# A decoder layer whose linear-attention values and gates become four Strassen column pairs

## The chip, the cores and the metric

The kernel runs on 1 core of one Trainium2 chip. The metric is the device time of one execution in microseconds (us).

## What is computed

One layer of a decoder trunk, 256 tokens, width 2048, all in float32. The input is normed and multiplied by one wide matrix `w_in`; its columns are the linear attention's parts, three groups of dilated attention and two gates.

```
h = RMSNorm(x)
z = h @ W_in          # GLA q, k (1024 each), v, output gate (2048 each), low-rank decay input (16),
                      # 9 x 1024 for the dilated groups, 2 x 2048 branch gates
A = GLA(q, k, v, log_sigmoid(lr @ w_gk_up + b_gk) / 16)      # 4 heads, dk 256, dv 512, chunks of 64
A = RMSNorm(A, per head) * silu(g)
Bm = DilatedAttn(h)                                           # 8 heads x 128 in 3 groups
x = x + (sigmoid(ga) * (A @ W_a) + sigmoid(gb) * (Bm @ W_b)) @ W_out
x = x + SwiGLU(RMSNorm(x))
out = RMSNorm(x)
```

## The kernel before

Every large product is done in float32 accuracy from a high and a low half: ScalarE rounds a piece of the weights to its high half `wh`, VectorE subtracts for the low half `wl` (`split`, L283), and TensorE adds three matmuls, high x high, high x low and low x high. The activations `h` are kept split in the same way (`HiLo`), transposed, in 16 k tiles of 128. 

The work is a list of jobs (`Job`, added by `win` and `add`), each a product of the 256 tokens with some columns of a weight matrix over all 16 k tiles. A job is cut into units, one weight DMA each, 1 MB as a rule, on SP's queue into a ring of three `raw` tiles; a unit is cut into sub-steps, each one split and its matmuls (`mains`). The main loop (L1105) takes the sub-steps in order: it issues the split four sub-steps ahead (`LA`, five ring pairs `wh`, `wl`), then the evacuation of the job that has just ended (`pending.evac`), then the job's hook for this sub-step (`pre`), one step of the side queue (`advance`), the sub-step's matmuls, and one more step of the side queue. So the order on each engine is fixed in program order.

The side queue holds generators, the attention heads above all (`gla_head`, L515; `dil_head`, L660): each `yield` hands the engine back to the main loop, so a head's matmuls stand between those of the jobs. `drain(tag)` runs the queue until no generator of that tag is left.

Kinds of job: "T" has the activations as the stationary operand and 512 (or fewer) weight columns moving, two token halves, 2 x 3 matmuls per k tile. "F" and "G" have the weights stationary and give a transposed result. "S" (`add_steps`, `step_mains`) takes two blocks of 512 columns at once, and two k tiles per step: a normal step is 8 products of 128 tokens x 512 columns (24 matmuls); a step listed in `fast` needs 7 products (21 matmuls) by Strassen's algorithm in Winograd's form, at the price of sums of weight blocks (`sums`, tile `t`) and of activation blocks (the forms, `x1_forms`). Before the change only the feed-forward part has "S" jobs: ten pairs of gate and up columns with steps 2, 4 and 6 of 8 fast.

Around the change the list of jobs runs (L742 to L763): the gate columns of heads 2 and 3 with the 16 low-rank columns behind them, 1040 columns as three "T" jobs of 348, 346 and 346; k and q of heads 2 and 3 ("F"); the values of heads 2 and 3; then the gates of heads 0 and 1, under which heads 2 and 3 run (tag "A"); k and q of heads 0 and 1; their values; then the dilated groups' jobs, under which heads 0 and 1 run (tag "B") and the bias table. The first job's sub-steps also stand among the transposes of the prologue (L1090), as x arrives in eight pieces.

Lines that the steps below name: L356 the matmuls of "T" and "F" jobs (L332 and L335 of "G"), L236 those of "S" jobs, L133 every ScalarE activation, L296 and L289 VectorE's part of a split, L195 to L199 its sums of weight blocks, L959 to L973 the sums at the end of an "S" job, L423 the prologue's transposes, L520 and L575 matmuls of a linear-attention head.

Of the kernel before, what the change touches and what calls it, by code (L numbers as in the profile page):

```python
# [10 lines left out]
F32 = mybir.dt.float32  # L11
# [12 lines left out]
NEG = -1e30  # L24

# [21 lines left out]
class Job:  # L47
# [14 lines left out]
    def __init__(self, kind, w, row0, nkt, col0, ncols, ktu, acts, evac, pre=None, pairs=None,  # L62
                 col1=None, fast=(), forms=None, turn=0):
        self.pairs = pairs
        self.col1, self.fast, self.forms = col1, fast, forms
        self.bank, self.turn = {}, turn
# [6 lines left out]
def trunk_layer(ctx: ExitStack, tc: tile.TileContext, x, attn_norm, w_in, w_gk_up, b_gk, gla_norm,  # L73
# [114 lines left out]
    def sums(sub):  # L188

        if sub.get("src") not in ("t13", "t24"):  # L190
            return
        b = raw_step(sub["unit"])
        if sub["src"] == "t13":
            t = sub["unit"]["t"] = env["fp"].tile([P, 4, 512], F32, name="t", tag="t")
            nc.vector.tensor_sub(t[:, 0:2], b[:, :, 1], b[:, 0])  # L195
        else:
            t = sub["unit"]["t"]
            nc.vector.tensor_sub(t[:, 2], b[:, 1, 1], t[:, 0])
            nc.vector.tensor_sub(t[:, 3], b[:, 1, 0], t[:, 2])  # L199
# [99 lines left out]
    def mains(sub, only=None, part=None):  # L299
# [6 lines left out]
        if not hasattr(job, "acc"):  # L306
# [146 lines left out]
    def view(key, slot, a, fresh=True):  # L453

        if key not in env:
            env[key] = block("z", slot).rearrange("p (a t) -> p a t", a=a)
        return env[key]
# [14 lines left out]
    def g_chunk(lo, hi, slots, base):  # L472

        def go(job):
            for a in range(2):
                c = lo
                while c < hi:
                    sc = env["rstd"][:, a:a + 1]
                    if c >= 1024:
                        act(lrn[:, a], job.acc[a][:, c - lo:hi - lo], AF.Copy, scale=sc)  # L480
                        c = hi
                        continue
                    j = c // 512
                    e = min(hi, (j + 1) * 512)
                    g = view(("g", base + j), slots[j], 2)
                    act(g[:, a, c - j * 512:e - j * 512], job.acc[a][:, c - lo:e - lo],
                                         AF.Silu, scale=sc)
                    c = e
        return go
# [10 lines left out]
    def evac_zf(key, slot):  # L500
        def go(job):
            scaled(job, view(key, slot, 4), "R")
        return go
# [11 lines left out]
    def gla_head(h, half):  # L515
# [94 lines left out]
        hl = hl_block("o", {2: 4, 3: 6, 0: 0, 1: 2}[h])  # L610
# [125 lines left out]
    def start_half(tag, heads):  # L736
        def go():
            for h in heads:
                push(tag, gla_head(h, tag))
        return go  # L740

    c0 = C_G + 1024  # L742
    for lo, hi in ((0, 348), (348, 694), (694, 1040)):
        ev = g_chunk(lo, hi, (0, 1), 2)
        if hi == 1040:
            def ev(job, f=ev):
                f(job)
                push("A", gla_lr())
        win("T", c0 + lo, hi - lo, ev)
    win("F", C_K + 512, 512, evac_zf(("k", "A"), 2))  # L750
    win("F", C_Q + 512, 512, evac_zf(("q", "A"), 3))
    win("T", C_V + 1024, 512, evac_t(("v", 2), 4))
    win("T", C_V + 1536, 512, evac_t(("v", 3), 5, start_half("A", (2, 3))))
    win("T", C_G, 512, g_chunk(0, 512, (6, 7), 0))
    win("T", C_G + 512, 512, g_chunk(512, 1024, (6, 7), 0))
    win("F", C_K, 512, evac_zf(("k", "B"), 8))
    win("F", C_Q, 512, evac_zf(("q", "B"), 9), {0: lambda: drain("A")})
    win("T", C_V, 512, evac_t(("v", 0), 0))

    def after_b():  # L760
        start_half("B", (0, 1))()
        push("bias", bias_table())
    win("T", C_V + 512, 512, evac_t(("v", 1), 1, after_b))  # L763


# [117 lines left out]
    FAST = (2, 4, 6)  # L883
    x1F = {}

    def x1_forms():

        yield from idle(1)
        for n, st in enumerate(FAST):
            t = x1T[st // 2].t[st % 2]  # L890
            a = env["fp"].tile([P, 2, S], F32, name="fa", tag="u0")
            f = env["fp"].tile([P, 4, P], F32, name="ff", tag="u1")
            nc.vector.tensor_add(a, t[:, :, 0].bitcast(F32), t[:, :, 1].bitcast(F32))
            nc.vector.tensor_add(f[:, 0], a[:, 0, P:], a[:, 1, P:])
            nc.vector.tensor_sub(f[:, 2], a[:, 0, 0:P], a[:, 0, P:])
            nc.vector.tensor_sub(f[:, 1], f[:, 0], a[:, 0, 0:P])
            nc.vector.tensor_sub(f[:, 3], a[:, 1, 0:P], f[:, 1])
            b = x1F[st] = block("o", n, F32R).rearrange("p (w f q) -> p w f q", w=2, f=4)
            act(b[:, 0], f, AF.Copy)
            nc.vector.tensor_sub(b[:, 1], f, b[:, 0].bitcast(F32))  # L900
            yield
            yield

    def ffn_norm_chunk(c):
# [5 lines left out]
        if c == 3:  # L910
# [3 lines left out]
            push("F", x1_forms())  # L914

    def evac_out(c):
        def go(job):
            for a in range(2):
                nc.vector.tensor_add(x1[c][:, a], job.acc[a], x1[c][:, a])
                junk = env["fp"].tile([P, 512], F32, name="junk", tag="u3")  # L920
# [33 lines left out]
    def evac_step1(job):  # L954

        u = job.u = [env["fp"].tile([P, 512], F32, name=f"u{i}", tag=f"u{i}") for i in range(4)]
        b = job.bank
        act(u[0], b["p1"], AF.Copy)
        nc.vector.tensor_add(u[1], u[0], b["p6"])  # L959
        nc.vector.tensor_add(u[2], u[1], b["p7"])  # L960
        nc.vector.tensor_add(u[1], u[1], b["p5"])
        nc.vector.tensor_add(u[3], u[2], b["p5"])

    def evac_step2(p):
        def go(job):
            u, b = job.u, job.bank
            z = env["fp"].tile([P, 2, 512], F32, name="sg", tag="sg", bufs=2)
            nc.vector.tensor_add(z[:, 0], u[0], b["p2"])
            act(z[:, 0], z[:, 0], AF.Silu, scale=env["rstd2"][:, 0:1])
            nc.vector.tensor_add(u[1], u[1], b["p3"])  # L970
            nc.vector.tensor_add(z[:, 1], u[2], b["p4"])
            act(z[:, 1], z[:, 1], AF.Silu, scale=env["rstd2"][:, 1:2])
            nc.vector.tensor_add(u[3], u[3], b["p8"])  # L973
            for a in range(2):
                nc.vector.scalar_tensor_tensor(z[:, a], u[1 + 2 * a], env["rstd2"][:, a:a + 1], z[:, a],
                                               op0=ALU.mult, op1=ALU.mult)
            turn_up(p, z, 2, 2 * job.turn)
        return go

    def evac_down(c, last):  # L980
        def go(job):
            for a in range(2):
                nc.vector.tensor_add(x1[c][:, a], job.acc[a], x1[c][:, a])
                if last:
                    junk = env["fp"].tile([P, 512], F32, name="junk", tag="u3")
# [13 lines left out]
    def fast_pair(p, turn):  # L999
        def start():  # L1000
            drain("F")
            drain("A")
        job = Job("S", w_ffn_in, 0, KT, 512 * p, 512, 2, x1_acts, evac_step2(p), {4: start}, None,
                  FF + 512 * p, FAST, lambda st: x1F[st], turn)
        add(job)
        job.pre[len(job.subs) - 2] = lambda: evac_step1(job)
# [26 lines left out]
    more = next(i for i, s in enumerate(subs) if s["job"].kind == "S") + LA + 1  # L1033
# [47 lines left out]
    def input_rstd():  # L1081
# [5 lines left out]
        env["R"] = row_bcast("R", env["rstd"])  # L1087

# [116 lines left out]
```

## Time and profile before

| | |
|---|---|
| median of 3 runs | 1864.06 us (1863.65 to 1865.05) |
| profiled execution | 1863.59 us, span 1861.5 us |
| TensorE (PE) busy | 1847.5 us, 9234 matmuls |
| VectorE (DVE) busy | 1197.6 us |
| ScalarE (ACT) busy | 913.2 us |
| granted TensorE clock, mean | 0.999 |

The span runs from the first to the last instruction of the profiled execution. Matmuls are pipelined: one's duration reaches into the next one's, so what a matmul costs in a row of them is the distance from its start to the next start, and of n equal matmuls that a row merges, (row's time - one's duration) / (n - 1). `x8` at a row's end is the number of instructions, a timeline's row begins with start and time in us, `[... <-X]` is what ended an engine's idle time before it.

### The profile page before, as it was taken

How to read it: one execution, taken by the hardware profiler on the slowest of the kernel's cores; microseconds unless marked ns; L12 is line 12 of the kernel's file. 1: busy time of each engine (PE TensorE's matmuls, PEld its weight loads, DVE VectorE, ACT ScalarE, POOL GpSimd, SP SyncE). 2: the span in 40 equal slices, each digit the busy share in tenths (PEclk: the TensorE clock that was granted, in tenths of full speed). 3: DMA queues.
4: the chain of work that ended last, by engine and by line, in shares of the span. 5: the costliest groups of instructions: out<-in, count | busy, mean ns of one | idle time of the engine just before them, and what ended most of it. 6: DMA issues, size and time to landing. Idle time of an engine off the chain costs nothing.

```text
span 1861.5 us, 23268 instructions
## 1 busy us (share of the span) xinstructions
PE 1847.5 (99%) x9234; PEld 1572.2 (84%) x9234; DVE 1197.6 (64%) x1394; ACT 913.2 (49%) x1144; POOL 22.3 (1%) x35
## 2 busy tenths in 40 slices
PE   8999999999999999999999999999999999999998
PEld 8988988888888888888888888888888888888887
DVE  6446646745665466655545556789647998559974
ACT  6446545544444444544444455555435555335553
POOL 0000000000000000000000000000000000000001
PEclk9999999999999999999999999999999999999999
DMA  7554455455555566466656655555655655545562
GB/s 253 205 195 167 159 187 176 162 182 186 179 176 181 192 182 209 147 199 207 205 201 218 234 182 180 192 193 204 219 188 189 217 183 205 201 161 203 202 236 103
DMA packets 208580, 356.33 MB, mean 191 GB/s; under 512 B 7403, under 2 KB 67879, under 8 KB 208472
## 3 DMA queue, kind: packets, MB, share of 16 engines
q1 hardware_dynamic: 203472, 346.19, 54.1%
q0 software_dynamic: 1728, 5.51, 1.4%
q10 hardware_dynamic: 3272, 3.16, 0.6%
q8 instruction: 72, 1.18, 0.2%
q14 instruction: 36, 0.29, 0.0%
HBM read 352.70 MB, written 2.13 MB: 191 GB/s over the span
## 4 chain that ended last, share of the span: by engine, by line
PE 99%; DMA 0%; DVE 0%; ACT 0%; SPq 0%; issue 0%; DVEq 0%; ACTq 0%
PE acc L356 51%; PE acc L236 12%; PE acc L332 10%; PE psb L356 6%; PE psa L236 5%; PE acc L335 5%; PE psb L236 5%; PE psa L672 1%; PE psb L717 0%; PE psa L593 0%; PE psa L818 0%; PE psb L575 0%; PE psb L682 0%; PE psb L719 0%; PE acc L818 0%; PE psa L693 0%
## 5 line engine op out<-in xcount | busy, mean ns | idle before, releaser
L133 ACT ACTIVATE wh<-raw 128x1024 fp32r<-128x1024 f32 (+3 forms) x614 | 625.8, 1026 | 633.6 <-PE acc L356 435.6
L296 DVE TENSOR_TENSOR wl<-raw,wh 128x1024 fp32r<-128x1024 f32 (+2 forms) x482 | 580.9, 1212 | 505.7 <-ACT wh L133 503.8
L356 PE MATMUL acc<-wh,h 128*128 128x512 f32 (+2 forms) x1536 | 469.8, 383 | 0.0
L356 PEld LDWEIGHTS acc<-wh,h 128*128 128x128 f32 x1536 | 286.6, 188 | 54.2 <-issue 1.3
L356 PE MATMUL acc<-wl,h 128*128 128x512 f32 (+2 forms) x768 | 292.9, 381 | 0.0
L332 PE MATMUL acc<-h,wh 128*128 128x512 f32 x768 | 196.4, 397 | 0.0
L356 PE MATMUL acc<-wh,z 128*128 128x512 f32 x600 | 187.8, 390 | 0.0
L289 DVE TENSOR_TENSOR wl<-raw,wh 128x1024 fp32r<-128x1024 f32 (+1 forms) x132 | 143.1, 1100 | 42.3 <-ACT wh L133 41.9
L356 PEld LDWEIGHTS acc<-wl,h 128*128 128x128 f32 x768 | 144.7, 188 | 25.5
L332 PEld LDWEIGHTS acc<-h,wh 128*128 128x128 f32 x768 | 138.5, 189 | 26.9 <-issue 0.7
L236 PE MATMUL acc<-wh,h 128*128 128x512 f32 x446 | 146.7, 390 | 0.0
L356 PEld LDWEIGHTS acc<-wh,z 128*128 128x128 f32 x600 | 112.6, 188 | 23.2
L356 PE MATMUL acc<-wl,z 128*128 128x512 f32 x300 | 116.7, 389 | 0.0
L335 PEld LDWEIGHTS acc<-h,wl 128*128 128x128 f32 x768 | 104.6, 190 | 7.8
L335 PE MATMUL acc<-h,wl 128*128 128x256 f32 x768 | 106.9, 282 | 0.0
L236 PEld LDWEIGHTS acc<-wh,h 128*128 128x128 f32 x446 | 83.7, 188 | 17.3
L356 PE MATMUL acc<-h,wh 128*128 128x256 f32 x512 | 92.5, 283 | 0.0
L236 PE MATMUL acc<-wl,h 128*128 128x512 f32 x223 | 86.8, 389 | 0.0
L133 ACT ACTIVATE wh<-t 128x1024 fp32r<-128x1024 f32 x51 | 54.1, 1060 | 58.4 <-DVE t L199 26.5
L356 PEld LDWEIGHTS acc<-h,wh 128*128 128x128 f32 x512 | 80.0, 192 | 0.2
L356 PE MATMUL acc<-wh,o 128*128 128x512 f32 x256 | 79.4, 389 | 0.0
L356 PE MATMUL psb<-wh,z 128*128 128x512 f32 (+1 forms) x248 | 75.8, 381 | 0.0
(276 smaller groups left out, 2308.6 us busy)
## 6 DMA issues: line engine op xcount, KB each, us to landing
raw<-in_w_in_dram SPq DMA_DIRECT2D x144, 1024.0 KB, 4.7
raw<-in_w_ffn_in_dram SPq DMA_DIRECT2D x160, 512.0 KB, 4.4
raw<-in_w_ffn_out_dram SPq DMA_DIRECT2D x44, 1024.0 KB, 5.0
raw<-in_w_branch_gla_dram SPq DMA_DIRECT2D x16, 1024.0 KB, 5.0
raw<-in_w_out_dram SPq DMA_DIRECT2D x16, 1024.0 KB, 4.9
raw<-in_w_branch_dil_dram SPq DMA_DIRECT2D x8, 1024.0 KB, 4.9
raw<-in_w_ffn_in_dram SPq DMA_DIRECT2D x8, 1024.0 KB, 4.7
raw<-in_w_in_dram SPq DMA_DIRECT2D x8, 692.0 KB, 4.0
```

The source lines that it names most:

```text
L133: nc.scalar.activation(o, i, func, **kw)
L236: nc.tensor.matmul(job.bank[pr["b"]], st, mv, start=pr["first"] and i == 0, stop=pr["last"] and i == 2, skip_group_check=True)
L289: nc.vector.tensor_sub(wl, src, wh.bitcast(F32))
L296: nc.vector.tensor_sub(wl[:, :k * n], src, wh[:, :k * n].bitcast(F32))
L332: nc.tensor.matmul(job.acc[j], wh[:, kk, c], hl.both(aj), start=ki == 0, stop=ki == job.nkt - 1, skip_group_check=True)
L335: nc.tensor.matmul(job.acc[j][:, 0:S], wl[:, kk, c], hl.hi(aj), start=False, stop=ki == job.nkt - 1, skip_group_check=True)
L356: nc.tensor.matmul(dst, st, mv, start=first and i == 0 and j % per_bank == 0, stop=last and i == 2, skip_group_check=True)
L672: nc.tensor.matmul(p1[:, g * 256:(g + 1) * 256], qk[g][:, 0, 128:256], qk[g][:, 1], start=g != 1, stop=True, skip_group_check=True)
```

## The change

The gates and the values of the linear attention, 4 x 1024 columns, become four "S" jobs (`win_fast`), each a pair of two heads' 512 columns, with steps 2, 4 and 6 of 8 fast as in the feed-forward part. The forms of h that they need (`act_forms`) are made once, under the second job. The 16 low-rank columns get a "T" job of their own: one unit, one sub-step, 16 k tiles x 2 token halves x 3 matmuls of 16 columns. The order is now: k, q of heads 2 and 3; low-rank; gates of heads 2 and 3, gates of heads 0 and 1, values of heads 2 and 3, values of heads 0 and 1; k, q of heads 0 and 1. Heads 2 and 3 start when the last value pair is done and run under k and q of heads 0 and 1 and the first dilated jobs; heads 0 and 1 start under the dilated jobs as before. Tiles in `z` and `o` get other places. The feed-forward part's "S" jobs are built by the same helper (`fast_job`): the sums of a pair's end stand in another order, two sums are made in place, and the weight sums live in two tiles `t13` and `t24` instead of one.

```diff
+    def act_forms(blocks, out, dst, tmp):
+        yield from idle(1)
+        for n, st in enumerate(FAST):
...
+            nc.vector.tensor_add(a, t[:, :, 0].bitcast(F32), t[:, :, 1].bitcast(F32))
+            nc.vector.tensor_add(f[:, 0], a[:, 0, P:], a[:, 1, P:])
+            nc.vector.tensor_sub(f[:, 2], a[:, 0, 0:P], a[:, 0, P:])
+            nc.vector.tensor_sub(f[:, 1], f[:, 0], a[:, 0, 0:P])
+            nc.vector.tensor_sub(f[:, 3], a[:, 1, 0:P], f[:, 1])
...
+            act(b[:, 0], f, AF.Copy)
+            nc.vector.tensor_sub(b[:, 1], f, b[:, 0].bitcast(F32))
+            yield
+            yield
+    def fast_job(w, col0, col1, acts, forms, turn, tile, dst, evac, pre):
+        def first(job):
+            c = job.c = dst()
+            b = job.bank
+            act(c[0], b["p1"], AF.Copy)
+            nc.vector.tensor_add(c[1], c[0], b["p6"])
+            nc.vector.tensor_add(c[2], c[1], b["p7"])
+            nc.vector.tensor_add(c[1], c[1], b["p5"])
+            nc.vector.tensor_add(c[3], c[2], b["p5"])
+        def second(job):
+            for i, n in ((0, "p2"), (2, "p4"), (1, "p3"), (3, "p8")):
+                nc.vector.tensor_add(job.c[i], job.c[i], job.bank[n])
+                evac(job, i)
+        job = Job("S", w, 0, KT, col0, 512, 2, acts, second, pre, None, col1, FAST, lambda st: forms[st], turn, tile)
+        add(job)
+        job.pre[len(job.subs) - 2] = lambda: first(job)
...
-        add(Job(kind, w_in, 0, KT, col, n, 8 if n <= 256 else 4, h_acts, evac, pre))
+        add(Job(kind, w_in, 0, KT, col, n, KT if n < 64 else 8 if n <= 256 else 4, h_acts, evac, pre))
...
+        def evac(job, i):
+            act(job.c[i], job.c[i], func, scale=env["rstd"][:, i // 2:i // 2 + 1])
+            if then and i == 3:
+                then()
+        fast_job(w_in, col, col + 512, h_acts, hF, turn, lambda t: block("o", int(t == "t24")), dst, evac, pre)
...
-    for lo, hi in ((0, 348), (348, 694), (694, 1040)):
...
-    win("F", C_K + 512, 512, evac_zf(("k", "A"), 2))
-    win("F", C_Q + 512, 512, evac_zf(("q", "A"), 3))
-    win("T", C_V + 1024, 512, evac_t(("v", 2), 4))
-    win("T", C_V + 1536, 512, evac_t(("v", 3), 5, start_half("A", (2, 3))))
-    win("T", C_G, 512, g_chunk(0, 512, (6, 7), 0))
-    win("T", C_G + 512, 512, g_chunk(512, 1024, (6, 7), 0))
-    win("F", C_K, 512, evac_zf(("k", "B"), 8))
-    win("F", C_Q, 512, evac_zf(("q", "B"), 9), {0: lambda: drain("A")})
-    win("T", C_V, 512, evac_t(("v", 0), 0))
-    win("T", C_V + 512, 512, evac_t(("v", 1), 1, after_b))
+    win("F", C_K + 512, 512, evac_zf(("k", "A"), 6))
+    win("F", C_Q + 512, 512, evac_zf(("q", "A"), 7))
+    win("T", C_LR, 16, evac_lr)
+    win_fast("g", (2, 3), (3, 5), C_G + 1024, 0, AF.Silu, {4: first_fast})
+    win_fast("g", (0, 1), (8, 9), C_G, 1, AF.Silu, {})
+    win_fast("v", (2, 3), (2, 4), C_V + 1024, 0, AF.Copy, {})
+    win_fast("v", (0, 1), (0, 1), C_V, 1, AF.Copy, {}, last_values)
+    win("F", C_K, 512, evac_zf(("k", "B"), ("o", 0)))
+    win("F", C_Q, 512, evac_zf(("q", "B"), ("o", 1), after_b))
...
+            if r == 0:
+                first = {3: lambda g=g: drain(("A2", "A2", "A3")[g])}
...
-    more = next(i for i, s in enumerate(subs) if s["job"].kind == "S") + LA + 1
+    more = next(i for i, s in enumerate(subs) if s["job"].w is w_ffn_in and s["job"].kind == "S") + LA + 1
```

`more` is the place from which on every sixth sub-step's split goes to a sixth pair of buffers; it stays in the feed-forward part.

TensorE's order, the gate columns of heads 2 and 3 before (`h_168` and the like are split tiles of h, `acc` a bank of PSUM):

```order
L356 MATMUL acc<-wl,h_168 128x346
L356 MATMUL acc<-wh,h_168 128x346 x2
L356 MATMUL acc<-wl,h_168 128x346
L356 MATMUL acc<-wh,h_168 128x346
L356 MATMUL acc<-wh,h_169 128x346
```

and now, at the end of the low-rank job and the start of the first pair (L272 is the matmul of an "S" job in the changed kernel, L392 that of the others):

```order
L392 MATMUL acc<-wh,h_319 128x16 x2
L392 MATMUL acc<-wl,h_319 128x16
L392 MATMUL acc<-wh,h_319 128x16
L272 MATMUL acc<-wh,h_119 128x512
L272 MATMUL acc<-wl,h_119 128x512
L272 MATMUL acc<-wh,h_119 128x512 x2
```

The 16 low-rank columns, which were part of the 346 wide matmuls, are now 96 matmuls by themselves ahead of the first pair.

ScalarE's order at that place now (`lrn` is the normed low-rank input, copied out of the bank):

```order
L134 ACTIVATE wh<-raw 128x1024 x2
L134 ACTIVATE wh<-raw 128x512
L134 ACTIVATE lrn<-acc,r_attn 128x16 x2
L134 ACTIVATE wh<-raw 128x1024
L537 COPY lrT<-psb 16x256
```

The copies stand behind the split of 512 columns for the first fast step. Before, they stood between the evacuations of a gate job.

VectorE's order at the end of the last value pair now (`z_2153` and `z_2154` hold the values of heads 0 and 1):

```order
L332 TENSOR_TENSOR wl<-raw,wh 128x1024 x2
L240 TENSOR_TENSOR z_2153<-z_2153,psa 128x512
L240 TENSOR_TENSOR z_2153<-z_2153,psb 128x512
L240 TENSOR_TENSOR z_2154<-z_2154,psa 128x512
L240 TENSOR_TENSOR z_2154<-z_2154,psb 128x512
L332 TENSOR_TENSOR wl<-raw,wh 128x1024
L553 SCALAR_TENSOR_TENSOR gk<-psb,ge 128x512
```

and TensorE's there (L544 is head 2's first matmul):

```order
L272 MATMUL psb<-wl,h_319 128x512
L272 MATMUL psb<-wh,h_319 128x512
L392 MATMUL acc<-h_119,wh 128x256 x2
L392 MATMUL acc<-h_119,wl 128x256
L544 MATMUL psb<-lrT,wgk 128x256 x2
L392 MATMUL acc<-h_120,wh 128x256 x2
```

Between the pair's last matmul and head 2's first stand the 24 matmuls of one sub-step of k; both sides use the banks `psb`.

## Rows read from the trace of the kernel before

**Rows 1.** The page: span, busy time by engine.
```profile
span 1861.5 us, 23268 instructions
...
PE 1847.5 (99%) x9234; PEld 1572.2 (84%) x9234; DVE 1197.6 (64%) x1394; ACT 913.2 (49%) x1144; POOL 22.3 (1%) x35
```
**Rows 2.** All waits of TensorE: what waited, for what, us in total, times, longest.
```profile
PE psb L1027 <- DMA grow<-in_attn_norm_dram: 3.8, 1, 3.8
PE psb L423 <- DMA o<-in_x_dram: 1.5, 1, 1.5
```
**Rows 3.** L356 from 38 to 54 us: count, shortest/median/longest ns, first and last start.
```profile
L356 PE MATMUL acc<-wh,h x69: 316/322/330, 37.7 to 53.9; 128*128 128x346 f32 x69
...
L356 PE MATMUL acc<-wl,h x34: 316/322/329, 37.9 to 53.6; 128*128 128x346 f32 x34
```
**Rows 4.** 512-column job's timeline; four pairs' busy (PE, PEld, DVE, ACT, POOL).
```profile
104.51 0.62 PE L356 MATMUL acc<-wh,h 128*128 128x512 f32 x2
...
114.04 0.62 PE L356 MATMUL acc<-wh,h 128*128 128x512 f32 x2
...
1403.40:1571.70 168.30, 168.30 (x756) 139.64 (x755) 149.87 (x165) 95.01 (x104) 0.00 (x0) 1.00 0.57 198
```
**Rows 5.** L575, a head's small matmuls: timeline, then durations of loads and matmuls.
```profile
162.48 1.06 PE L575 MATMUL psb<-qe,ke 128*128 128x128 f32 x8
...
163.92 0.68 PE L575 MATMUL psb<-qe,kd 128*64 128x64 f32 x8
...
L575 PEld LDWEIGHTS psb<-qe,ke x32: 187/192/192, 162.3 to 343.8; 128*128 128x128 f32 x32
L575 PE MATMUL psb<-qe,ke x32: 271/275/275, 162.5 to 343.9; 128*128 128x128 f32 x32
L575 PEld LDWEIGHTS psb<-qe,kd x32: 132/138/138, 163.9 to 345.0; 128*64 128x64 f32 x32
L575 PE MATMUL psb<-qe,kd x32: 222/222/270, 163.9 to 345.0; 128*64 128x64 f32 x32
```
**Rows 6.** Busy by engine, clock, DMA share, GB/s from 4 to 7 us; DMA issues.
```profile
4.00:7.00 3.00, 1.38 (x6) 0.92 (x6) 0.92 (x3) 1.51 (x3) 0.00 (x0) 1.00 1.01 327
...
T<-ftab ACTq DMA_DIRECT2D x8, 384.0 KB, 5.8
```
**Rows 7.** ScalarE by form: count, busy us, mean ns of one, idle before.
```profile
L133 ACT ACTIVATE wh<-raw 128x512 fp32r<-128x512 f32 x30 | 18.6, 622 | 13.2 <-PE psb L356 5.0 <-PE acc L236 4.7 <-PE psb L236 3.5
...
L133 ACT ACTIVATE lrn<-acc,r_attn 128x16 f32<-128x16 f32 x2 | 0.5, 274 | 0.0
```
**Rows 8.** VectorE's timeline at the end of a feed-forward pair.
```profile
1274.42 1.22 DVE L289 TENSOR_TENSOR wl<-raw,wh 128x1024 fp32r<-128x1024 f32 x1
1275.56 0.68 DVE L968 TENSOR_TENSOR sg<-u,psa 128x512 f32<-128x512 f32 x1
...
1277.95 1.41 DVE L975 SCALAR_TENSOR_TENSOR sg<-u,r_ffn,sg 128x512 f32<-128x512 f32 x2
```
**Rows 9.** TensorE's timeline at both ends, its weight loads, clock behind its last matmul.
```profile
6.83 1.09 PE L423 MATMUL psb<-ident,o 128*128 128x128 f32 x4 [1.49 <-DMA o<-in_x_dram]
...
8.43 0.79 PE L356 MATMUL acc<-wh,h 128*128 128x348 f32 x2
...
12.36 0.48 PE L356 MATMUL acc<-wh,h 128*128 128x348 f32 x2
...
7.50 0.34 PEld L356 LDWEIGHTS acc<-wh,h 128*128 128x128 f32 x1
...
10.22 0.19 PEld L356 LDWEIGHTS acc<-wl,h 128*128 128x128 f32 x1
...
1852.64 0.28 PE L356 MATMUL psa<-wh,z 128*128 128x256 f32 x1
...
1853.00:1856.50 3.50, 0.00 (x0) 0.00 (x0) 2.22 (x9) 1.64 (x5) 0.00 (x0) 1.00 0.00 0
1856.60:1861.00 4.40, 0.00 (x0) 0.00 (x0) 0.39 (x1) 0.00 (x0) 0.00 (x0) 0.50 0.63 238
```

More of the change, by code (lines that the diff above doesn't have):

```diff
@@ L62, in __init__ @@
     def __init__(self, kind, w, row0, nkt, col0, ncols, ktu, acts, evac, pre=None, pairs=None,
-                 col1=None, fast=(), forms=None, turn=0):
+                 col1=None, fast=(), forms=None, turn=0, tile=None):
         self.pairs = pairs
         self.col1, self.fast, self.forms = col1, fast, forms
-        self.bank, self.turn = {}, turn
+        self.bank, self.turn, self.tile = {}, turn, tile
         self.kind, self.w, self.row0, self.nkt = kind, w, row0, nkt
@@ L470, in trunk_layer, with evac_lr @@
     nc.vector.memset(inside[:, ::64], 0.0)
[L472 to L489, printed above, removed]
+    def evac_lr(job):
+        for a in range(2):
+            act(lrn[:, a], job.acc[a], AF.Copy, scale=env["rstd"][:, a:a + 1])
+        push("L", gla_lr())
     def evac_t(key, slot, then=None):
@@ L498, in evac_t, with evac_zf @@
         return go
-    def evac_zf(key, slot):
+    def evac_zf(key, slot, then=None):
         def go(job):
             scaled(job, view(key, slot, 4), "R")
+            if then:
+                then()
         return go
@@ new lines, in start_half, with win_fast, dst @@
+    def start_half(half, heads):
+        for h in heads:
+            push(f"{half}{h}", gla_head(h, half))
+    hF = {}
+    def win_fast(name, heads, slots, col, turn, func, pre, then=None):
+        def dst():
+            v = [view((name, h), slot, 2) for h, slot in zip(heads, slots)]
+            return [v[i % 2][:, i // 2] for i in range(4)]
+        def evac(job, i):
+            act(job.c[i], job.c[i], func, scale=env["rstd"][:, i // 2:i // 2 + 1])
+            if then and i == 3:
+                then()
+        fast_job(w_in, col, col + 512, h_acts, hF, turn, lambda t: block("o", int(t == "t24")), dst, evac, pre)
@@ L766, in push_heads, with drain_b @@
+    win_fast("g", (0, 1), (8, 9), C_G, 1, AF.Silu, {})
[3 more added lines that the diff above has]
+    win("F", C_Q, 512, evac_zf(("q", "B"), ("o", 1), after_b))
+    def drain_b():
+        for t in ("B0", "B1", "bias"):
+            drain(t)
     def push_heads(r):
@@ L952, in evac_fup @@
         return go
[L954 to L978, printed above, removed]
     def evac_down(c, last):
@@ L1002, in start, with tile, dst, evac @@
             drain("A")
[L1003 to L1006, printed above, removed]
+        def tile(name):
+            return env["fp"].tile([P, 1024], F32, name=name, tag=name)
+        def dst():
+            z = env["sg"] = env["fp"].tile([P, 2, 512], F32, name="sg", tag="sg", bufs=2)
+            u = [env["fp"].tile([P, 512], F32, name=f"u{i}", tag=f"u{i}") for i in range(2)]
+            return z[:, 0], u[0], z[:, 1], u[1]
+        def evac(job, i):
+            a = i // 2
+            r = env["rstd2"][:, a:a + 1]
+            if i % 2 == 0:
+                act(job.c[i], job.c[i], AF.Silu, scale=r)
+                return
+            nc.vector.scalar_tensor_tensor(job.c[2 * a], job.c[i], r, job.c[2 * a], op0=ALU.mult, op1=ALU.mult)
+            if a:
+                turn_up(p, env["sg"], 2, 2 * turn)
+        fast_job(w_ffn_in, 512 * p, FF + 512 * p, x1_acts, x1F, turn, tile, dst, evac, {4: start})
     def down(p0, n, last):
```

72 lines of the change are left out of this document (26 added, 46 removed).

## The prediction

> **What bounds the kernel now.** I read the page first: TensorE is busy 1847.5 of 1861.5 us, VectorE 64% and ScalarE 49% of them [rows 1]. A busy share counts pipelined matmuls as whole, so the second view is TensorE's waits: the whole list is two, 3.8 and 1.5 us, both for DMAs in the first 7 us [rows 2]. Behind them TensorE never waits for anything, not even under the linear attention's heads. So the third view is the distance from one matmul's start to the next, on the timeline; the kernel's time is the number of matmuls times that distance, plus the start and some 9 us after the last matmul. VectorE and ScalarE make the splits that TensorE consumes, and matter only where they come late.
>
> The profiled execution took 1863.59 us, 0.47 under the median of the three runs (1864.06). I sum differences against it and put them on the median. A measurement here can tell about 0.2% (3.7 us) from no change.
>
> **Distances.** 346 columns: 69 + 34 = 103 matmuls start between 37.7 and 53.9 us, 16.2 / 102 = 0.159 us each [rows 3]. 512 columns: 42 matmuls start from 104.51 up to 114.04, in groups of three, 9.53 / 42 = 0.227 [rows 4]. The slope between 346 and 512 columns is (0.227 - 0.159) / 166 = 0.41 ns per column, the remainder 17 ns.
>
> **What goes and what comes.** The order shows it exactly: 192 matmuls of 346 and 96 of 348 columns go, 156 of 512 and 96 of 16 columns come; all other shapes keep their number.
> - Gone: 288 x 0.159 = 45.8 us.
> - Come, wide: without Strassen 192 would be needed for what the 288 did; 12 fast steps save 3 each. 156 x 0.227 = 35.4 us.
> - Come, narrow: 96 matmuls of 16 columns for the low-rank input, which used to ride along in the 346 wide ones. Each has a full 128x128 stationary tile, and each matmul of this kernel has a weight load of its own (9234 and 9234 [rows 1]). No row shows a full tile against so few columns. By its columns alone, 17 ns and 16 x 0.41, one takes 0.024; at the other end it can't be slower than a 346-wide one at the same clock, 0.159. Nearest by the stationary tile are the heads' 128-column matmuls: eight last 1.06 us, (1.06 - 0.275) / 7 = 0.112 apart; with a 64-column tile against 64 columns eight last 0.68, (0.68 - 0.222) / 7 = 0.065 [rows 5]. In these rows tile and columns shrink together. But the weight load itself lasts 192 ns for 128 columns and 138 for 64 [rows 5], 54 ns more for 64 more, so a full tile takes about 108 ns to stream, and the next load starts when the matmul before it starts. I take 0.112: 10.8 us.
>
> Sum: -45.8 + 35.4 + 10.8 = **+0.4 us**. The narrow job eats what the pairs save; the balance would be even at 0.108 per narrow matmul.
>
> **What lies around it.**
> - Start. The first job now has 512 columns where it had 348, so its first unit of two k tiles is 512 KB (2 x 128 x 512 x 4 bytes) instead of 348 and stands in SP's queue ahead of the x piece on which TensorE waits its 1.5 us. DMA moved 327 GB/s there [rows 6]: 164 KB more is +0.5 us (0 to 1). Later units are larger too, but a sub-step of the first job then takes 24 matmuls of 256 columns (0.017 + 256 x 0.00041 = 0.12 us each, 2.9 in all) instead of 12 x 0.159 us, so TensorE needs them later.
> - The low-rank input's one DMA brings 64 bytes per row in 2048 pieces; it is issued three units ahead, some 14 us of matmuls, while the nearest, 384 KB in 1 KB pieces, landed in 5.8 us [rows 6]. Nothing.
> - First pair. Its second product waits for the bank that the low-rank job leaves; the order puts the two copies that empty it behind a split of 512 on ScalarE: 0.62 + 2 x 0.27 = 1.16 us [rows 7], against 3 x 0.227 = 0.68 of the first product. +0.5 (0 to 1).
> - The pairs' VectorE work. In the four feed-forward pairs VectorE was busy 149.87 of 168.30 us without TensorE waiting [rows 4]. The new pairs ask for less: no gated product (1.41 us a pair [rows 8]) and no transposed block to split. They lack the sixth pair of split buffers that the feed-forward part borrows. A fast step needs 1.22 + 2 x 0.68 for its sums and 0.68 + 3 x 1.22 for its splits, 6.9 us by duration, against 21 matmuls, 4.8 us; but the normal step beside it needs 2.4 against 5.4, so four sub-steps of lead carry it. Nothing; what it costs without that lead is a rival. The forms of h (three times five short sums and two long ones) fall under the second job, where VectorE has 1.22 us of work per 2.9: nothing. ScalarE's table loads get fewer: nothing, it is hidden.
> - Heads. 21 steps each, two per sub-step: the A heads need 42 and get 16 + 16 under K and Q, and 10 of the 48 under the first six dilated jobs; the B heads and the bias table fit in the rest and the next values job. So no drain empties a queue at one go, and SP's and POOL's queues are passed by nothing that matters. But head 2's first matmul stands behind the first sub-step of K (2.9 us) and needs a bank that the last pair's second group of sums empties: behind one split 1.22 + 4 x 0.68 = 3.9 us [rows 8]. +1.0 (0 to 2).
> - The feed-forward sums are only reordered, same number: nothing. The same for the rest behind it.
>
> Sum at a steady clock: 0.4 + 0.5 + 0.5 + 1.0 = +2.4 us.
>
> **The clock.** In the narrow job TensorE streams 16 columns every 0.112 us, about 7 ns of them (0.41 a column), for 11 us on end. Nothing in the trace before is so thin for more than a microsecond, and the granted clock is 1.00 from 10 us to the end of the matmuls. It does move twice. At the start two 348-column matmuls take 0.79 us at 8.43 and 0.48 at 12.36: 1.2, then 2.4 GHz; ahead of the rise TensorE had done transposes, and from 7.5 on dense matmuls [rows 9]. After the last matmul (1852.64) the granted clock is still 1.00 up to 1856.5, and 0.50, 1.2 GHz, behind it [rows 9]. Weight loads are slower at the low clock too: 0.34 us at 7.50 against 0.19 at 10.22 [rows 9]. Whether so thin a stretch counts as work no row tells. I hold it for likelier than not that it doesn't: what the rise followed was full streaming. Price, with the delays of these rows: about 3.7 us of the job, 33 matmuls, at full speed, 63 at 2 x 0.112 = 14.1 us, so 17.8 instead of 10.8, +7.0; then the first pair begins at half speed for some 2.7 us (as from 7.50 to 10.22), +1.3; the first pair's wait (0.5) vanishes in it. Bounds: +3 if the fall comes late in the job; +13 if the whole job and the stretch behind it are slow. Sum: 2.4 - 0.5 + 8.3 = +10.2.
>
> The Trainium skill (TensorE: Matmul & The Clock Gate, "A second HAM failure mode: psum-queue depth-cycling") tells of a kernel whose many short pauses between matmuls, none long, were enough to send the clock back and forth. By it the fall would come, with the +10.2 above; by the granted clock of this trace, never below 1.00 between its ends, the sum would stay at +2.4.
>
> **Forecast and rivals.**
> - A, forecast, 0.50: narrow job at one weight load per matmul and the clock falls in it: 1864.06 + 10.2 = **1874.3 us** (its own range 1867 to 1879).
> - B, 0.31: the same, the clock holds: 1866.5 (1863 to 1869). For it: weight loads keep TensorE occupied all through the job. I count 0.27 of it as no measurable change.
> - C, 0.15, the other side: the narrow matmul takes its columns' time, the load going on beneath its neighbours. At 0.024 the job is 2.3 us: -45.8 + 35.4 + 2.3 + 2.0 = -6.1, 1858.0 us. It decides below some 0.05 us per matmul; there the sum passes -3.7. For it: nothing in the rows holds a full load against fewer than 128 columns. Against it: the 54 ns per 64 columns of load, and loads that never start ahead of the matmul before them.
> - D, 0.04: the new pairs are not fed, for want of the sixth buffer pair: 12 fast steps x (6.9 - 4.8) = 25 us at most, half of it hidden by the lead: 1879.
>
> On C the Trainium skill (same page, "Back-to-back issue gap") gives about 25 ns for matmuls of up to 64 columns, which would make the job 2.4 us and the time C's. None of the rows goes below 0.065 us, so no run here shows it.
>
> Chances: faster C, 0.15; within 0.2% most of B, 0.27; slower A, D and the rest of B, 0.58. The range leaves out most of C and the upper ends of A and D: 1862 to 1879.
>
> **What would show it.** In the profile after: the 16-column matmuls at their line, first to last start: 17 us (A), 10.7 (B), 2.3 (C). Granted clock of the stretch of that job and the 5 us behind: below 1.00 in A, 1.00 in B and C. The first matmul of the pair's second product waits for ScalarE about 0.5 us in B. TensorE's waits at the start some 0.5 us longer; head 2's first matmul waiting for VectorE about 1 us. The four new pairs at 0.227 us per matmul and with no wait; a list of waits for the splits there would be D. I am wrong in the main if the narrow matmuls are well under 0.1 us apart, or if the four pairs stall.

## The result and the profile after

The changed kernel takes **1874.29 us** (median of 4 runs, 1873.72 to 1875.20) where the kernel before takes 1864.22 (4 runs beside them): 1.0054 of it, 95% interval 1.0037 to 1.0072. It is slower, by 10.1 us; the forecast was 1874.3. The profiled execution took 1874.11 us, 10.5 more than that of before.

The page of the changed kernel, span and busy time, answers to [rows 1]:

```profile
span 1872.1 us, 23391 instructions
...
PE 1856.2 (99%) x9198; PEld 1574.6 (84%) x9198; DVE 1272.5 (68%) x1497; ACT 929.4 (50%) x1160; POOL 22.1 (1%) x35
```

TensorE has 36 matmuls fewer than before and is busy 8.7 us longer. Its waits, all of them, answer to [rows 2]:

```profile
PE psb L1038 <- DMA grow<-in_attn_norm_dram: 3.7, 1, 3.7
PE psb L459 <- DMA o<-in_x_dram: 2.5, 1, 2.5
PE psb L544 <- DVE z L240: 0.7, 1, 0.7
```

The wait for x is 1.0 us longer, and one wait is new, 0.7 us in front of head 2. The other 8.8 us are in no wait of a matmul. They are in the low-rank job and just behind it. First its 16-column matmuls by form (count, shortest/median/longest ns, first and last start; weight loads are PEld):

```profile
L392 PEld LDWEIGHTS acc<-wh,h x64: 192/333/334, 59.3 to 76.4; 128*128 128x128 f32 x64
L392 PE MATMUL acc<-wh,h x64: 175/361/362, 59.4 to 76.5; 128*128 128x16 f32 x64
```

The weight load has two durations, 192 ns at the shortest and 333 as the median, the two that [rows 9] show at the two ends of the clock's rise. Busy time of the engines in five stretches around the job (PE, PEld, DVE, ACT, POOL, then the granted clock, the DMAs' share and GB/s):

```profile
50.00:59.30 9.30, 9.30 (x80) 9.30 (x79) 7.25 (x16) 3.16 (x4) 0.00 (x0) 1.00 0.49 192
59.40:62.70 3.30, 3.30 (x33) 3.30 (x31) 2.28 (x7) 1.94 (x3) 0.00 (x0) 1.00 0.78 271
62.70:76.50 13.80, 13.80 (x67) 13.80 (x67) 3.23 (x4) 0.58 (x1) 0.00 (x0) 0.50 0.25 88
76.50:79.80 3.30, 3.30 (x9) 2.50 (x10) 1.83 (x2) 0.96 (x3) 0.00 (x0) 0.50 0.00 0
79.80:85.00 5.20, 5.20 (x25) 4.23 (x24) 2.52 (x3) 2.15 (x3) 0.00 (x0) 1.00 0.00 0
```

The granted clock is 1.00 in the first 3.3 us of the job, 0.50 (1.2 GHz) in the other 14.0 and for the first 3.1 us of the first pair, then 1.00 again. PE and PEld are busy throughout: TensorE never stands idle, it loads tiles. The timeline of the job and of the seam behind it (start, duration):

```profile
59.38 0.17 PE L392 MATMUL acc<-wh,h 128*128 128x16 f32 x1
...
59.86 0.37 PE L392 MATMUL acc<-wh,h 128*128 128x16 f32 x2
...
62.20 0.37 PE L392 MATMUL acc<-wh,h 128*128 128x16 f32 x2
...
63.03 0.57 PE L392 MATMUL acc<-wh,h 128*128 128x16 f32 x2
...
76.47 0.36 PE L392 MATMUL acc<-wh,h 128*128 128x16 f32 x1
76.69 0.77 PE L272 MATMUL acc<-wh,h 128*128 128x512 f32 x1
...
79.81 0.39 PE L272 MATMUL acc<-wl,h 128*128 128x512 f32 x1
```

The job lasts from 59.38 to 76.69, 17.3 us. At full speed 21 narrow matmuls start from 59.86 up to 62.20, 0.111 us each; behind the fall 63 start from 63.03 up to 76.47, 0.213 each. Seven wide matmuls then start between 76.69 and 79.81, in 3.1 us instead of 7 x 0.227 = 1.6: 1.5 us more.

The four pairs follow without a pause. The end of the last on the timeline:

```profile
244.16 0.39 PE L272 MATMUL psb<-wh,h 128*128 128x512 f32 x1
244.39 0.40 PE L392 MATMUL acc<-h,wh 128*128 128x256 f32 x2
```

Busy times of the whole stretch, which answer to [rows 4]:

```profile
76.60:245.00 168.40, 168.40 (x742) 139.23 (x742) 143.16 (x152) 97.22 (x108) 0.00 (x0) 0.99 0.54 194
```

Their 732 matmuls take 244.39 - 76.69 = 167.7 us; without the 1.5 of the slow clock that is 0.227 each, the distance of before. VectorE is busy 143.16 us in this stretch, under the 149.87 of the feed-forward pairs.

### The profile page after: what moved, and what is told of

Same layout as the page of the kernel before. It is cut to its first block, busy times and chain, and to the rows that moved or that the text cites. A ratio compares the mean times of both kernels' runs of the same rounds, so it can differ in the third digit from the quotient of the medians.

```text
span 1872.1 us, 23391 instructions
## 1 busy us (share of the span) xinstructions
PE 1856.2 (99%) x9198; PEld 1574.6 (84%) x9198; DVE 1272.5 (68%) x1497; ACT 929.4 (50%) x1160; POOL 22.1 (1%) x35
## 4 chain that ended last, share of the span: by engine, by line
PE 99%; DVE 0%; DMA 0%; ACT 0%; issue 0%; SPq 0%; DVEq 0%; ACTq 0%
PE acc L392 42%; PE acc L272 17%; PE acc L368 9%; PE psa L272 7%; PE psb L272 7%; PE psb L392 6%; PE acc L371 5%; PE psa L694 1%; PE psb L739 0%; PE psa L617 0%; PE psa L857 0%; PE psb L599 0%; DMA raw<-in_w_in_dram 0%; PE psb L704 0%; PE psb L741 0%; PE acc L857 0%
## 5 line engine op out<-in xcount | busy, mean ns | idle before, releaser
L134 ACT ACTIVATE wh<-raw 128x1024 fp32r<-128x1024 f32 (+1 forms) x607 | 618.2, 1027 | 580.8 <-PE acc L392 333.0
L332 DVE TENSOR_TENSOR wl<-raw,wh 128x1024 fp32r<-128x1024 f32 x411 | 500.7, 1226 | 403.4 <-ACT wh L134 401.1
L392 PE MATMUL acc<-wh,h 128*128 128x512 f32 (+1 forms) x1024 | 317.8, 387 | 0.0
L325 DVE TENSOR_TENSOR wl<-raw,wh 128x1024 fp32r<-128x1024 f32 (+1 forms) x196 | 212.5, 1106 | 73.9 <-ACT wh L134 73.2
L392 PEld LDWEIGHTS acc<-wh,h 128*128 128x128 f32 x1024 | 195.4, 194 | 38.9 <-issue 1.9
L272 PE MATMUL acc<-wh,h 128*128 128x512 f32 x642 | 211.7, 392 | 0.0
L392 PE MATMUL acc<-wl,h 128*128 128x512 f32 (+1 forms) x512 | 197.3, 385 | 0.0
L392 PE MATMUL acc<-wh,z 128*128 128x512 f32 x600 | 187.8, 390 | 0.0
L272 PEld LDWEIGHTS acc<-wh,h 128*128 128x128 f32 x642 | 121.2, 189 | 25.4 <-ACT lrn L134 0.3
L392 PEld LDWEIGHTS acc<-wh,z 128*128 128x128 f32 x600 | 112.7, 188 | 23.2
L272 PE MATMUL acc<-wl,h 128*128 128x512 f32 x321 | 125.4, 391 | 0.0
L392 PE MATMUL acc<-wl,z 128*128 128x512 f32 x300 | 116.7, 389 | 0.0
L392 PEld LDWEIGHTS acc<-wl,h 128*128 128x128 f32 x512 | 99.4, 194 | 18.1
L272 PE MATMUL psb<-wh,h 128*128 128x512 f32 x298 | 107.0, 389 | 0.0
L392 PE MATMUL acc<-h,wh 128*128 128x256 f32 x512 | 95.0, 287 | 0.0
L272 PE MATMUL psa<-wh,h 128*128 128x512 f32 x244 | 86.3, 390 | 0.0
L392 PEld LDWEIGHTS acc<-h,wh 128*128 128x128 f32 x512 | 80.8, 194 | 1.0 <-ACT wh L134 0.3
```

Of the source, the lines that this page charges most:

```text
L134: nc.scalar.activation(o, i, func, **kw)
L272: nc.tensor.matmul(job.bank[pr["b"]], st, mv, start=pr["first"] and i == 0, stop=pr["last"] and i == 2, skip_group_check=True)
L325: nc.vector.tensor_sub(wl, src, wh.bitcast(F32))
L332: nc.vector.tensor_sub(wl[:, :k * n], src, wh[:, :k * n].bitcast(F32))
L392: nc.tensor.matmul(dst, st, mv, start=first and i == 0 and j % per_bank == 0, stop=last and i == 2, skip_group_check=True)
```

## Experiments

All kernels are edits of the changed kernel. The theory under test: the loss is the low-rank job, by one weight load per narrow matmul and by the clock that falls in it. The rivals: the clock falls for some other reason at that place, or the pairs themselves cost more than they save.

**e1_spread: the same 96 matmuls, spread.** They stand in sixes among the matmuls of q of heads 2 and 3, and write to a bank `psb`.

```diff
...
+        for i in range(sub["k"]) if sub["job"] is env["qa"] else ():
+            mains(dict(sub, k0=sub["k0"] + i, k=1, w=[t[:, i:i + 1] for t in sub["w"]]))
+            mains(dict(lr, k0=sub["k0"] + i, k=1, w=[t[:, sub["k0"] + i:sub["k0"] + i + 1] for t in lr["w"]]))
...
```

> The changed kernel with its 96 narrow matmuls spread: six after every 24/2 = 12 matmuls of the second job (q of heads 2 and 3) instead of 96 in one stretch; their bank is one of psb. Nothing else. My theory (a narrow matmul costs one weight load, 0.112 us, and it is the unbroken thin stretch that lowers the clock): granted clock 1.00 all through, the 96 cost 10.7 us instead of 17.1, and the slow 3.3 us behind them (1.65 lost) go: 1874.3 - 6.4 - 1.7 = 1866.3 us. Rival 1 (so many small matmuls lower the clock however they stand): 0.50 in a part of the second job, 1874 or more, since wide matmuls then run at half speed too. Rival 2 (the load hides beneath wide neighbours): 96 at 0.02 to 0.03, 1858 us.

Measured: 1866.26 us (1865.86 to 1866.69, 10 runs), 1.0010 of before (1.0001 to 1.0019). Its timeline at one six:

```profile
49.95 0.73 PE L394 MATMUL psb<-z,h 128*128 128x16 f32 x6
50.54 0.49 PE L394 MATMUL acc<-h,wh 128*128 128x256 f32 x2
50.87 0.28 PE L394 MATMUL acc<-h,wl 128*128 128x256 f32 x1
```

Busy times and clock of q with all the sixes (columns as above):

```profile
34.00:59.00 25.00, 25.00 (x217) 25.00 (x215) 14.96 (x26) 11.13 (x14) 0.00 (x0) 1.00 0.61 216
```

Six start within 50.54 - 49.95 = 0.59 us, and the pair of matmuls behind them takes 0.33 instead of the usual 0.24: 0.68 for six, 0.113 each. So the narrow matmul costs its 0.11 wherever it stands, and the clock stays at 1.00 when the narrow ones are not among themselves. The 8.0 us between this and the changed kernel is the clock's price, 6.5 in the job and 1.5 behind it by the rows above; the waits at the start (1.9 for 2.5) and in front of head 2 (1.0 for 0.7) differ by some tenths besides. That rules out the other reasons at the place of the first pair, which is unchanged here.

**e2_pad256: the same job with 256 columns.** Of these, 16 are used; the stationary tiles, their number and the order stay.

```diff
...
-    win("T", C_LR, 16, evac_lr)
+    win("T", C_LR, 256, evac_lr)
```

> The changed kernel with the low-rank job widened from 16 to 256 columns: the same 96 matmuls, stationary tiles and place, 16 times the moving columns; the 240 further columns are those of the dilated part and are left unused. It adds 1.9 MB of weights and four splits. My theory (the columns are too few for the clock, the load sets the pace): granted clock 1.00, 96 x 0.120 = 11.5 us instead of 17.1, the slow 3.3 us behind go: 1874.3 - 5.6 - 1.7 = 1867.0 us, up to 0.5 more if the first pair's second product then waits for its bank. Rival (the fall comes from the place in the program, or from full stationary tiles in quick turn, not from the columns): clock 0.50 there again, the matmuls at 0.23 us, 1876 us or more.

Measured: 1866.40 us (1865.64 to 1867.41, 10 runs), 1.0012 of before (1.0003 to 1.0021). The job's rows by form:

```profile
L392 PEld LDWEIGHTS acc<-wh,h x64: 191/192/193, 58.5 to 69.9; 128*128 128x128 f32 x64
L392 PE MATMUL acc<-wh,h x64: 282/283/284, 58.6 to 70.0; 128*128 128x256 f32 x64
```

Busy times and clock of the job and of what follows:

```profile
59.00:70.00 11.00, 11.00 (x94) 11.00 (x94) 9.95 (x14) 5.49 (x6) 0.00 (x0) 1.00 0.43 136
70.00:75.00 5.00, 5.00 (x26) 4.03 (x25) 2.69 (x3) 2.27 (x5) 0.00 (x0) 1.00 0.92 360
```

Sixteen times the columns, and the job is 5.8 us shorter: 95 distances in 11.4 us, 0.120 each. With e1_spread it separates the two prices: the matmuls' own 11 us are paid in both, the clock in neither. TensorE's waits are the three of the changed kernel, with 2.0 us for x: no wait of the first pair, at full clock either.

**e3_no_strassen: the four pairs as eight plain jobs.** The low-rank job stays.

```diff
-    win_fast("g", (2, 3), (3, 5), C_G + 1024, 0, AF.Silu, {4: first_fast})
...
+    for h, slot in ((2, 3), (3, 5), (0, 8), (1, 9)):
+        win("T", C_G + 512 * h, 512, evac_g(h, slot))
...
```

> The changed kernel with the four pairs as eight plain T jobs (no fast steps, no forms of h, no sums); order, low-rank job and heads stay. My theory: the pairs save 12 fast steps x 3 matmuls x 0.227 = 8.2 us, and the head's wait of 0.7 us goes, the clock falls as before: 1874.3 + 8.2 - 0.7 = 1881.8 us. Rival (the pairs give what they save back to sums, forms and bank waits, and the narrow job is only a part of the loss): 1874 to 1877.

Measured: 1880.99 us (1880.84 to 1881.93, 4 runs), 1.0090 of before (1.0077 to 1.0104). The clock around the low-rank job:

```profile
62.60:76.50 13.90, 13.90 (x67) 13.90 (x67) 0.15 (x1) 0.00 (x0) 0.00 (x0) 0.50 0.23 77
76.50:79.50 3.00, 3.00 (x8) 2.39 (x8) 1.23 (x1) 1.38 (x3) 0.00 (x0) 0.50 0.00 0
```

The fall is there without any pair behind it, so it belongs to the job. The first narrow matmul and the first of K:

```profile
59.16 0.18 PE L392 MATMUL acc<-wh,h 128*128 128x16 f32 x1
...
252.36 0.40 PE L392 MATMUL acc<-h,wh 128*128 128x256 f32 x2
```

From one to the other pass 193.2 us, in the changed kernel 244.39 - 59.38 = 185.0. So the 36 matmuls that Strassen saves are worth 8.2 us, 0.227 each, as expected. Against that stands head 2's wait of 0.7 us, which is gone from the list here: 7.5 was expected in all. The medians differ by 6.7; a start that is 0.2 us earlier is a part of the 0.8 that is lacking, and the other 0.6, between medians of four runs each, stays open.

**e4_ride: the low-rank columns ride along again.** The gates of heads 2 and 3 are three jobs of 348, 346 and 346 as before; three pairs remain, with turns 0, 1, 0 (the turn says in which banks a pair's products lie).

```diff
...
+    for lo, hi in ((0, 348), (348, 694), (694, 1040)):
+        win("T", C_G + 1024 + lo, hi - lo, g_chunk(lo, hi))
...
-    win("T", C_LR, 16, evac_lr)
...
+    win_fast("g", (0, 1), (8, 9), C_G, 0, AF.Silu, {4: first_fast})
+    win_fast("v", (2, 3), (2, 4), C_V + 1024, 1, AF.Copy, {})
+    win_fast("v", (0, 1), (0, 1), C_V, 0, AF.Copy, {}, last_values)
```

> The low-rank columns ride along again: the gates of heads 2 and 3 as the three T jobs of 348, 346 and 346 at the start, as before the change; the other three column sets stay fast pairs in the changed order. No narrow matmuls. My theory: against the kernel before, 9 fast steps x 3 x 0.227 = 6.1 us less, start as before, clock 1.00 throughout: 1864.2 - 6.1 = 1858.1 us, up to 1 more for a head's wait. Rival (the new order of the heads, the forms and sums cost several us that the clock's fall now covers): 1862 to 1865.

Measured: 1864.97 us (1862.49 to 1866.53, 11 runs), 1.0002 of before (0.9993 to 1.0011): 6.9 us above what was expected, a miss. Two new waits of TensorE:

```profile
PE acc L392 <- DVE z L240: 3.1, 1, 3.1
...
PE acc L272 <- DVE z L486: 0.6, 1, 0.6
```

Its timeline behind the longer one:

```profile
234.31 0.77 PE L392 MATMUL acc<-h,wh 128*128 128x256 f32 x2 [3.10 <-DVE z L240]
...
237.01 0.57 PE L392 MATMUL acc<-h,wh 128*128 128x256 f32 x2
237.40 0.29 PE L392 MATMUL acc<-h,wl 128*128 128x256 f32 x1
```

With turn 0 the last pair's last products lie in the `acc` banks, which K of heads 0 and 1 needs at once; VectorE empties them in the pair's second group of sums. TensorE stands for 3.1 us and afterwards runs at half speed until 237.4. Whether these waits are all of the miss was left to the next run.

**e7_ride_turn: e4_ride with turns 1, 0, 1.**

```diff
-    win_fast("g", (0, 1), (8, 9), C_G, 0, AF.Silu, {4: first_fast})
+    win_fast("g", (0, 1), (8, 9), C_G, 1, AF.Silu, {4: first_fast})
```

(The other two pairs are then as in the changed kernel.)

> As e4_ride, but the three pairs take their banks in the other order (turns 1, 0, 1), so that K of heads 0 and 1 finds its banks free behind the last pair. Theory (e4_ride missed 1858.1 by a wait of 3.1 us for those banks, the clock's fall behind it, 1.7, and 0.6 in front of the first pair): all three go, 1858.1 + 0.7 to 0.9 for head 2's wait as in the changed kernel = 1859 us. Rival (the banks' wait only moves into one of the pairs, or e4_ride's miss lies in the slow rise of the clock at the start): 1862 to 1865.

Measured: 1859.56 us (1858.38 to 1860.62, 9 runs), 0.9975 of before (0.9965 to 0.9984), within 0.6 of the theory. The waits for the banks are gone; of those that hang on the pairs one is left, beside 0.5 and 0.3 us elsewhere:

```profile
PE psb L557 <- DVE z L240: 0.7, 1, 0.7
```

So the turn was 5.4 of the 6.9 us that e4_ride missed by, and head 2's wait, for which the forecast had left room, 0.7 of the rest. Three pairs alone, without a narrow job, are faster than the kernel before.

**e5_stack: the low-rank product stacked and transposed.**

```diff
...
+        if job.kind == "L":
+            job.acc = ps_b()
+            for ki in range(job.nkt):
+                hl, aj = job.acts(ki)
+                nc.tensor.matmul(job.acc[0:32], sub["w"][:, ki], hl.both(aj), start=ki == 0, stop=ki == job.nkt - 1)
...
-    win("T", C_LR, 16, evac_lr)
+    win("L", C_LR, 16, evac_lr)
```

`sub["w"]` holds the high and the low half side by side, `hl.both(aj)` both halves of h, 512 columns. VectorE adds the halves of the result that belong to h, and `wgk`, held twice, those that belong to the weights. The result is transposed already, so the two transposes that the narrow job's result needs go too.

> The low-rank product transposed and stacked: its high and low half stand side by side in one stationary tile of 32 columns, and the activations' high and low half (512 columns) move through it, so 16 matmuls of 512 columns take the place of 96 of 16. Theory (the narrow matmuls cost a load each and, by their thinness, the clock): 16 x 0.227 = 3.6 us for the job's 17.1, no fall of the clock, so 1874.3 - 17.1 - 1.6 + 3.6 = 1859.2 us, up to 1 us more because the first pair's second product then waits for the bank of q. Rival (the 0.45 of the clock's loss belongs to the start of the pair, not to the narrow job): the clock falls all the same, 1861 to 1864. The sum now also has the product low x low in it, which the three products leave out.

Measured: 1859.62 us (1859.12 to 1860.66, 11 runs), 0.9975 of before (0.9966 to 0.9984). The job on the timeline:

```profile
58.67 3.86 PE L351 MATMUL psb<-h,wh 128*32 128x512 f32 x16
```

The new wait behind it, from the list of TensorE's waits:

```profile
PE acc L272 <- DVE z L499: 0.8, 1, 0.8
```

Busy times and clock of the stretch:

```profile
58.00:62.00 4.00, 4.00 (x22) 2.28 (x22) 2.97 (x8) 1.95 (x3) 0.00 (x0) 1.00 0.64 212
62.00:66.00 4.00, 3.23 (x15) 2.24 (x14) 4.00 (x6) 1.48 (x3) 0.00 (x0) 1.00 0.33 90
```

The job takes 3.7 us in place of 17.3, the clock holds, and all four pairs are kept. The wait for q's evacuation, which the long narrow job had covered, comes out.

**e8_stack_banks and e10_stack_banks_start.** The first is e5_stack with q of heads 2 and 3 in banks that the first pair does not use; the second also lets the first two units bring one k tile each.

```diff
+    jobs[-1].pairs = [2]
```

```diff
-            u0, k = u1, 2 if not jobs[1:] and u1 < 4 else min(job.ktu, job.nkt - u1)
+            u0, k = u1, (1 if u1 < 2 else 2) if not jobs[1:] and u1 < 4 else min(job.ktu, job.nkt - u1)
```

> As e5_stack, but q of heads 2 and 3 writes into banks that the first pair does not use. Theory: the first pair's wait for q's evacuation goes, about 1 us: 1858.3. Rival (there is no such wait, or it moves to the low-rank product): as e5_stack, within 0.5 us.

> As e8_stack_banks, and the first job's first two units bring one k tile each (256 KB), so that less stands in SP's queue ahead of the pieces of x. Theory (the start costs +1.0 us since the first unit is 512 KB where it was 348): the wait at the start falls from 2.5 us to 1.7 or less and the time to about 1857.5. Rival (the queue is not what the x piece waits for): 1858.3, unchanged.

Measured: e8_stack_banks 1858.51 us (1858.09 to 1859.21, 6 runs), 0.9970 of before (0.9958 to 0.9981); e10_stack_banks_start 1858.65 us (1858.21 to 1859.36, 6 runs), 0.9971 (0.9959 to 0.9982). The first did what was expected: the list no longer has the wait for q's evacuation. No version has a lower median; the second's is the same within the noise. There the wait at the start fell as expected, but the time did not. That wait in e8_stack_banks and in e10_stack_banks_start:

```profile
PE psb L472 <- DMA o<-in_x_dram: 2.2, 1, 2.2
```

```profile
PE psb L472 <- DVE h L462: 1.5, 1, 1.5
```

The start of TensorE in e8_stack_banks:

```profile
8.40 0.78 PE L405 MATMUL acc<-h,wh 128*128 128x256 f32 x2
...
10.59 0.40 PE L405 MATMUL acc<-h,wh 128*128 128x256 f32 x2
...
12.37 0.60 PE L472 MATMUL psa<-ident,o 128*128 128x128 f32 x4
```

and in e10_stack_banks_start:

```profile
7.70 0.78 PE L405 MATMUL acc<-h,wh 128*128 128x256 f32 x2
...
10.41 1.05 PE L472 MATMUL psa<-ident,o 128*128 128x128 f32 x4
...
11.96 0.48 PE L405 MATMUL acc<-h,wh 128*128 128x256 f32 x2
```

The main matmuls begin 0.70 us earlier, but full speed comes at 11.96 instead of 10.59, and the transposes of the next x piece, which take 0.60 us per four in the one, take 1.05 in the other. So the x piece does come earlier when less stands ahead of it in the queue; TensorE then waits for VectorE's `h` instead. In these two profiles the later full speed took the gain back: the same 24 matmuls and 8 transposes are done at 13.16 us in e8_stack_banks and at 13.47 in e10_stack_banks_start. Why the rise came later is not settled: in both kernels TensorE was occupied on end until it came.

## Why the prediction was right

The forecast was case A, and each of its terms can be held against a row.

- **Narrow matmuls.** The distance was taken as 0.112 us, from heads' matmuls with a full tile and 128 columns. Until the clock falls the job makes 0.111; spread out it makes 0.113 (e1_spread). With the same full tile 16 and 128 columns have one distance, so there the load sets it and not the columns. Rival C, where the load would go on beneath its neighbours, needed under 0.05 and is out. The Trainium skill (TensorE: Matmul & The Clock Gate, "Back-to-back issue gap") has about 25 ns for isolated matmuls of up to 64 columns, and says that such a figure leaves the weight loads out; here, with a full tile loaded for each, the runs show 0.11 us.
- **Clock.** The job was put at 17.8 us and the slow stretch behind it at 1.3; measured 17.3 and 1.5. The fall came after 3.3 us and not 3.7, but a slow narrow matmul takes 0.213 us and not 0.224. The clock's price was put at +8.3; by the rows it is 17.3 - 10.8 + 1.5 = 8.0. Between the changed kernel and the two in which the clock holds stand 8.0 us (e1_spread) and 7.9 (e2_pad256, whose matmuls take 0.7 us more in all). Their times, 1866.3 and 1866.4, lie at rival B's (1866.5), the sum for a clock that holds, though not each of B's terms is in them. The Trainium skill (TensorE: Matmul & The Clock Gate, "A second HAM failure mode: psum-queue depth-cycling"), which the prediction named, tells of short idle times between groups of matmuls. This fall is not that one: the trace has no pause in the job, no wait of TensorE, and PE busy 13.80 of 13.80 us.
- **Wide matmuls.** 0.227 each in the four pairs, no wait. Rival D (the pairs starve for want of a sixth pair of buffers) is out. Strassen's steps alone save 8.2 us in their stretch (e3_no_strassen).
- **First pair's wait, a term that was misread.** Taken as 0.5, then as vanishing under the slow clock. There is none in the list, but the slow clock is not the reason: e2_pad256 has the same copies behind the job, a clock of 1.00, and no such wait. The four `acc` banks are taken in turn (`ps_acc`, four buffers): two for k, two for q, one for the low-rank job. So the pair's second product gets a bank of q, and only its fourth that of the low-rank job, 9 x 0.227 = 2.0 us after the pair's start, where the copies need 1.16. The sum did not suffer, because the forecast had added the 0.5 and taken it off again; rival B kept it. What does follow a short job is another wait, of 0.8 us, for the bank that q's evacuation frees (e5_stack); under the long job that evacuation was done in time.
- **Start, the term that was mis-sized.** "164 KB more is +0.5 us (0 to 1)" measured +1.0, at the end of its bounds. It moves from run to run: the seven other kernels whose first unit has two k tiles show 1.9 to 2.2 us with 512 columns and 1.2 with 348 (e4_ride, e7_ride_turn), against 2.5 and 1.5 in the two main profiles. So 0.4 to 1.3, with 0.8 in the middle. In e1_spread and e5_stack what ended it was VectorE's `h`, not the DMA. The larger first unit has a second price that the list does not hold, as it is a weight load that waits. ScalarE's and the load's rows in the changed kernel:

```profile
6.96 1.06 ACT L134 ACTIVATE wh<-raw 128x1024 fp32r<-128x1024 f32 x1 [0.91 <-DMA raw<-in_w_in_dram]
```

```profile
9.33 0.29 PEld L392 LDWEIGHTS acc<-h,wl 128*128 128x128 f32 x1 [0.42 <-DVE wl L332]
```

ScalarE waits for the weights, the split ends later, and the first matmul with a low half starts 0.90 us after the first two main ones (8.43 to 9.33), where e8_stack_banks takes 0.57: 0.3 us more.
- **Head 2.** Predicted 1.0, measured 0.7, for the sums of the last pair, as named. VectorE's timeline there:

```profile
245.68 1.23 DVE L332 TENSOR_TENSOR wl<-raw,wh 128x1024 fp32r<-128x1024 f32 x1 [0.43 <-ACT wh L134]
246.82 0.68 DVE L240 TENSOR_TENSOR z<-z,psa 128x512 f32<-128x512 f32 x1
247.42 0.68 DVE L240 TENSOR_TENSOR z<-z,psb 128x512 f32<-128x512 f32 x1
```

Behind the split and the sum that frees `psb` (ends 248.10) head 2's first matmul starts, at 248.16; it needed the second of the four sums, not the fourth, as the prediction had counted.

The sum of the measured terms is -45.8 + 35.4 + 17.3 + 1.5 + 1.0 + 0.7 = +10.1 us, for 10.5 between the two profiled executions. With the 0.3 us of the first split it is 10.4. By the distances the main matmuls run at half speed from 8.43 to some 11.5 here, and before from 7.5 to 10.2 at the latest [rows 9], so the start may hold the last tenth too. That the median lies 0.01 us from the forecast is chance: the start came 0.5 higher, or 0.8 with the first split, and the clock and head 2 some 0.6 lower than they were put.

## What to carry to other kernels

Before columns are cut out of a product into a job of their own, count its matmuls by their weight loads, not by their columns: here 96 of 16 columns cost 10.8 us at full clock, more than the 8.2 that Strassen's steps saved, and 17.3 with the clock that they brought down, which cost another 1.5 behind them. A TensorE that is 100% busy on both of its rows can still be losing half its clock, so read the granted clock stage by stage, and give such a job few loads and many columns (16 matmuls of 512 columns did it in 3.7 us). A wait under a long job comes out when the job is shortened: look at the banks on either side.

## What the runs showed of the hardware that was not expected

- A job with sixteen times the columns through the same stationary tiles was faster: 11.5 us with 256 columns at 0.120 each, 17.3 with 16, because the granted clock stayed at 1.00 in the one and was 0.50 in most of the other.
- The clock fell to 0.50 on an engine that had no idle time by any row, with matmuls and weight loads back to back; the load's median duration went from 192 to 333 ns with it.
- A pause of 3.1 us between dense matmuls (e4_ride) was followed by half speed, for another 3.1 us; behind one of 0.8 us (e5_stack) the clock stayed at 1.00. Two of e4_ride's eleven executions took 1862.49 and 1862.80 us at a mean clock of 0.999, the others 1864.45 or more at 0.997 or 0.998; so the fall may not come in every execution, but only one was profiled.
- Main matmuls that begin 0.7 us earlier at the start brought nothing, as full speed came 1.4 us later (e10_stack_banks_start).
- The half speed at the start stands in the distances only: two matmuls of 256 columns take 0.43 us there and 0.24 later, while the granted clock reads 1.00. The changed kernel's row:

```profile
8.40:11.40 3.00, 2.88 (x13) 2.58 (x12) 2.52 (x4) 1.78 (x3) 0.00 (x0) 1.00 1.04 381
```
